# Differential attention: the heads' split on GpSimd, the second projection spread over two more softmax steps, finished heads turned first, turns two units apart

## The chip, the cores and the metric

The kernel runs on one core of a Trainium2 chip. The core has five engines with queues of their own: TensorE (PE; its weight loads are shown apart as PEld), VectorE (DVE), ScalarE (ACT), GpSimd (POOL) and SyncE (SP), and 16 DMA engines. The metric is the time of one execution on the device in microseconds; the time of a kernel is the median of its runs, and beside it one execution is profiled.

## The reference

A trunk of four layers over 512 tokens of width 1024 in fp32. The mixers are S5, gated linear attention, differential attention and S5 again; behind each stands a SwiGLU feed-forward network, and each block begins with an RMS norm. Only the third mixer, differential attention, is touched here:

```python
def diff_attn_mixer(h, positions, w_qkv, lam_q1, lam_k1, lam_q2, lam_k2, subln_g, w_o, lambda_init):
    q, k, v = jnp.split(h @ w_qkv, 3, axis=-1)
    q = partial_rope(q.reshape(bsz, seq, 2 * DIFF_HEADS, DIFF_HD), positions) * DIFF_HD ** -0.5
    k = partial_rope(k.reshape(bsz, seq, 2 * DIFF_HEADS, DIFF_HD), positions)
    v = v.astype(f32).reshape(bsz, seq, DIFF_HEADS, 2 * DIFF_HD)
    ...
        s = jnp.einsum('bqhd,bkhd->bhqk', qb, k)
        mask = chunk_id[:, None, None, :] <= qcid[:, None, :, None]
        p = jax.nn.softmax(jnp.where(mask, s, NEG_INF), axis=-1)
        p = p.reshape(bsz, DIFF_HEADS, 2, Q_BLOCK, seq)
        a = p[:, :, 0] - lam * p[:, :, 1]
        return jnp.einsum('bhqk,bkhd->bqhd', a, v)
    ...
    o = o * lax.rsqrt(jnp.mean(o * o, axis=-1, keepdims=True) + 1e-5) * subln_g.astype(f32)
    o = o * (1.0 - lambda_init)
    return o.reshape(bsz, seq, D_MODEL).astype(h.dtype) @ w_o
```

There are 8 heads, each with two softmaxes over 64-wide queries and keys and one 128-wide value; four query tiles of 128 rows each.

## The kernel before, in words

**Precision.** A large matmul runs on operands that are split into a high part in fp32r and a low part, the value less its high part: `mm3` (L394 to L396) multiplies high by high, high by low and low by high into one PSUM bank. Three such matmuls of 512 columns are a *unit* here. Weights arrive by DMA in `wst`; ACT casts the high part (L366) and DVE subtracts the low part (L374), both into a buffer `whl`. There are five `whl` buffers.

**The stage.** `diff()` first projects q, k and v of heads 0 to 3 (`project(0, z)`, z = 0, 1, 2). Then 32 softmax steps follow, i = 0 to 31; `j, t = divmod(i, 4)` are the head and its query tile. On PE, whose queue takes the work in the order of the code, one step is

- `turned(i)`: four transposes aTp of the finished softmax (L2279), which ACT copies to aT (L2281);
- `prepare(j + 1)` at t = 0, which issues nothing on PE;
- `scores(i + 2)`: four matmuls into the two banks s (L2257); DVE adds the mask and takes the minimum (L2261), ACT exponentiates (L2265), DVE divides and subtracts the two softmaxes (L2267, L2268, L2272) into pr;
- a finished head's `done`, if one is due: transposes oTp (L2312), split by ACT (L514) and DVE (L515) into oT;
- some units, then `values(i)`: op (L2289), copied by ACT into o_s (L2292) and squared into `junk` (L2294), and some units more.

The units are those of `units` at first: q, k and v of heads 4 to 7, 96 in all. A finished block of q or k is scaled by ACT into qtm (L2195) and rotated by DVE (ro, L2200 to L2206), and a *turn* is queued that is due 6 units later: four transposes qTp (L2211) and ACT's copy into qk (L2212). When `units` are used up, `last` follows: columns 0 to 511 of the output projection, 32 units. Columns 512 on of the first two token tiles run behind step 31, with four weight blocks `w1` that are loaded and split in steps 26 and 29. In step i, n holds how many units run ahead of `values` and behind it.

**prepare(j + 1)** splits the queries and keys of the next head: high part by ACT (L2231), low part by DVE (L2232), into `hl`, of which there is one buffer (head 1 borrows a `whl`). Eight DMAs on POOL's queue then lay the pieces out as qs (L2239) and ks (L2240). Of qs there are two buffers; a head's qs waits until scores of the head two before it are through.

**normalised(j)**, after a head's last step: DVE makes q2 (L2301, L2302), POOL raises it to the power −1/2 (rs, L485), and DVE scales the four tiles of o_s (L2305). oTp needs these.

**back(d)** is a DMA on POOL's queue that restores half of the residual x into vall (L2340).

**Order.** PE's order is that of the code. On ACT, DVE and POOL a scheduler sets the order, and each engine works its own queue in order: what waits at its head holds all behind it. PSUM has two banks for the transposes and op (tp), two for s and four for acc.

Of the kernel before, what the change touches and what calls it, by code (L numbers as in the profile page):

```python
# [11 lines left out]
F32 = mybir.dt.float32  # L12
# [4 lines left out]
ALU = mybir.AluOpType  # L17
# [269 lines left out]
class Trunk:  # L287
# [1841 lines left out]
    def diff(self, l, left):  # L2129
        nc, i = self.nc, self.i  # L2130
        v = nc.vector
        w, wo = i["diff_w_qkv"][0], i["diff_w_o"][0]
        self.hand(mybir.EngineType.PE)
        with self.tc.tile_pool(name="diff", bufs=1) as p:
# [39 lines left out]
            queue, clock = [], [0]  # L2174

            def run(units, n=None):

                while n is None or n:
                    if next(units, units) is units:
                        break  # L2180
                    clock[0] += 1
                    while queue and queue[0][0] <= clock[0]:
                        queue.pop(0)[1]()
                    n = n and n - 1

            def rest():
                while queue:
                    queue.pop(0)[1]()

            def project(hf, z):  # L2190
                qk = qks[hf]

                def evac(t, ps):
                    q = self.np_.tile([P, 512], F32, tag=("h", "hh")[t % 2], name="qtm", bufs=2)
                    nc.scalar.mul(q[:], ps[:], r[:, t : t + 1])  # L2195
                    s3 = ps[:].rearrange("p (h d) -> p h d", d=64)
                    q3 = q[:].rearrange("p (h d) -> p h d", d=64)
                    ro = p.tile([P, 2, 8, 16], F32, tag="ro", name="ro", bufs=2)
                    c2 = cos2[:, t].unsqueeze(1).broadcast_to([P, 8, 16])
                    v.tensor_tensor(ro[:, 0], s3[:, :, 0:16], c2, op=ALU.mult)  # L2200
                    for y in range(2):
                        s1 = sin2[:, t, y * 8 : y * 8 + 8].unsqueeze(1).broadcast_to([P, 8, 8])
                        v.tensor_tensor(  # L2203
                            ro[:, 1, :, y * 8 : y * 8 + 8], s3[:, :, 8 - 8 * y : 16 - 8 * y], s1, op=ALU.mult
                        )
                    v.tensor_tensor(q3[:, :, 0:16], ro[:, 0], ro[:, 1], op=ALU.add)  # L2206

                    def turn():
                        tp = self.tp("qTp")
                        for j in range(4):  # L2210
                            nc.tensor.transpose(tp[:, j], q[:, j * P : (j + 1) * P], self.ident[:])  # L2211
                        nc.scalar.copy(qk[:, z, :, t * P : (t + 1) * P], tp[:])  # L2212

                    queue.append((clock[0] + 6, turn))

                def evac_v(t, ps):
                    nc.scalar.mul(vall[0][:, t, hf * 512 : (hf + 1) * 512], ps[:], r[:, t : t + 1])

                if z == 2 and not vall:
                    vall.append(self.xp.tile([P, NT, D], F32, tag="x", name="vall"))  # L2220
                yield from self.gemm_units(stat, w, KT, z * D + hf * 512, evac_v if z == 2 else evac)

            ready, kept = {}, {}

            def prepare(j):


                room, bufs, tag = (self.wp, 5, "whl") if j == 1 else (p, 1, "hl")
                hl = room.tile([P, 2, 2, SEQ], F32R, tag=tag, name="hl", bufs=bufs)
                src = qks[j // 4][:, :, j % 4]  # L2230
                nc.scalar.copy(hl[:, 0], src)  # L2231
                v.tensor_tensor(hl[:, 1], src, hl[:, 0].bitcast(F32), op=ALU.subtract)  # L2232
                qs = p.tile([P, 2, SEQ], F32R, tag="qs", name="qs", bufs=2)
                ks = self.wp.tile([P, 2, 2, SEQ], F32R, tag="whl", name="ks", bufs=5)
                for m in range(2):
                    rows = slice(m * 64, (m + 1) * 64)
                    for z in range(2):
                        to = slice(z * 64, (z + 1) * 64)
                        self.nc.gpsimd.dma_start(qs[to, m], hl[rows, z, 0])  # L2239
                        self.nc.gpsimd.dma_start(ks[to, m], hl[rows, :, 1])  # L2240
                ready[j] = qs, ks
                st = self.sp.tile([P, 2, NT], F32, tag="st", name="st")
                o_s = p.tile([P, NT, P], F32, tag="o_s", name="o_s", bufs=2)
                kept[j] = st, o_s
# [30 lines left out]
            def turned(i):  # L2275
                a = soft.pop(i)
                tp = self.tp("aTp")
                for kt in range(4):
                    nc.tensor.transpose(tp[:, kt], a[:, kt * P : (kt + 1) * P], self.ident[:])  # L2279
                aT = p.tile([P, 4, P], F32, tag="aT", name="aT", bufs=2)  # L2280
                nc.scalar.copy(aT[:], tp[:])  # L2281
                return aT
# [37 lines left out]
            units = project(0, 0)  # L2320
            run(units)
            tables()
            units = project(0, 1)
            run(units)
            units = project(0, 2)
            run(units, 8)
            rest()
            prepare(0)
            run(units)

            def projections():
                for z in range(3):
                    yield from project(1, z)
# [4 lines left out]
            def back(d):  # L2338

                nc.gpsimd.dma_start(vall[0][:, :, d * 512 : (d + 1) * 512], xdv[:, :, d * 512 : (d + 1) * 512])  # L2340
# [6 lines left out]
            units, last = projections(), self.gemm_units(so, wo, KT, 0, evac0)  # L2347
            done, w1 = {}, []
# [4 lines left out]
            run(units, 2)  # L2353
            for i in range(32):
                j, t = divmod(i, NT)
                if i == 15:
                    run(units)
                    rest()
                src, n = (units, (3, 3)) if i < 15 else (last, (1, 1))
                if i in (15, 28, 31):  # L2360
                    n = (0, 0)
                elif i == 29:
                    n = (0, 2)
                aT = turned(i)
                if t == 0 and j < 7:
                    prepare(j + 1)
                if i < 30:
                    scores(i + 2)
                if i in done:
                    done.pop(i)()  # L2370
                run(src, n[0])
                values(i, aT)
                run(src, n[1])
                if i in (16, 31):
                    back(i // 31)
                if i in (26, 29):
                    w1 += [self.wb(wo, kb, 512) for kb in ((0, 2) if i == 26 else (4, 6))]
                if t == 3:
                    done[i + (2 if j in (6, 7) else 3)] = normalised(j)
            self.x = vall[0]  # L2380
# [95 lines left out]
```

## Time and profile before

| | |
|---|---|
| median of 3 runs | 2307.91 us (2306.17 to 2310.44) |
| the profiled execution | 2306.32 us |
| its span in the profile | 2304.6 us |
| the 32 softmax steps | from 1248.95 us on; step 31 begins at 1417.97 us |
| granted clock in the stage | 1.00 |

Times within the profile count from the start of the span, in us. A row of the timeline gives start, duration, engine, line, operation and tiles; brackets at its end give how long the engine stood idle before it and what ended that. The beginnings of the aTp rows mark the steps; a step is as long as PE needs for its matmuls and for what it has to wait for.

### The profile page before, as it was taken

How to read it: one execution, taken by the hardware profiler on the slowest of the kernel's cores; microseconds unless marked ns; L12 is line 12 of the kernel's file. 1: busy time of each engine (PE TensorE's matmuls, PEld its weight loads, DVE VectorE, ACT ScalarE, POOL GpSimd, SP SyncE). 2: the span in 40 equal slices, each digit the busy share in tenths (PEclk: the TensorE clock that was granted, in tenths of full speed). 3: DMA queues.
4: the chain of work that ended last, by engine and by line, in shares of the span. 5: the costliest groups of instructions: out<-in, count | busy, mean ns of one | idle time of the engine just before them, and what ended most of it. 6: DMA issues, size and time to landing. Idle time of an engine off the chain costs nothing. (4 is left out here: it accounts for less than half of the span.)

```text
span 2304.6 us, 37230 instructions
## 1 busy us (share of the span) xinstructions
PE 2218.9 (96%) x14847; PEld 1967.2 (85%) x14847; DVE 1569.8 (68%) x2430; ACT 1120.4 (49%) x1865; POOL 280.3 (12%) x386
## 2 busy tenths in 40 slices
PE   5889999999999999999999999999999899999997
PEld 3778979898877799998987787999999788989996
DVE  7873887776624469777745675876766964967674
ACT  5634645454452456555535675744534224635342
POOL 1000140512000010101002131111000100101000
PEclk8999999999999999999999999999999899999999
DMA  4246666664422457766337365886641546767521
GB/s 86 40 111 187 142 179 167 173 170 110 120 74 73 130 140 191 188 160 174 92 115 154 89 147 148 212 224 144 167 100 46 144 143 162 178 170 171 155 78 64
DMA packets 295319, 317.83 MB, mean 138 GB/s; under 512 B 72205, under 2 KB 235337, under 8 KB 294890
## 3 DMA queue, kind: packets, MB, share of 16 engines
q1 hardware_dynamic: 232906, 234.23, 34.1%
q0 software_dynamic: 62240, 81.22, 19.1%
q8 instruction: 117, 1.92, 0.4%
q14 instruction: 56, 0.46, 0.1%
HBM read 283.54 MB, written 16.65 MB: 130 GB/s over the span
## 5 line engine op out<-in xcount | busy, mean ns | idle before, releaser
L374 DVE TENSOR_TENSOR whl<-wst,whl 128x1024 fp32r<-128x1024 f32 x272 | 331.4, 1222 | 255.7 <-ACT whl L366 254.7
L366 ACT CAST whl<-wst 128x1024 fp32r<-128x1024 f32 x272 | 284.0, 1050 | 316.4 <-PE acc L396 227.8
L561 PE MATMUL a<-side,whl 128*128 128x256 f32 x3168 | 382.9, 277 | 4.0 <-DVE whl L374 3.0
L561 PEld LDWEIGHTS a<-side,whl 128*128 128x128 f32 x3168 | 370.3, 188 | 6.3 <-DVE whl L374 4.1
L394 PE MATMUL acc<-whl,act 128*128 128x512 f32 x704 | 278.3, 396 | 1.4 <-DVE x L544 1.4
L396 PE MATMUL acc<-whl,act 128*128 128x512 f32 x704 | 274.7, 390 | 0.0
L395 PE MATMUL acc<-whl,act 128*128 128x512 f32 x704 | 274.6, 390 | 0.0
L561 PE MATMUL c<-side,whl 128*128 128x256 f32 x2112 | 254.0, 277 | 1.2 <-DVE whl L374 1.2
L561 PEld LDWEIGHTS c<-side,whl 128*128 128x128 f32 x2112 | 246.6, 188 | 1.8 <-DVE whl L374 1.8
L374 DVE TENSOR_TENSOR whl<-slot,whl 128x1024 fp32r<-128x1024 f32 x107 | 130.5, 1222 | 70.1 <-ACT whl L366 70.1
L394 PEld LDWEIGHTS acc<-whl,act 128*128 128x128 f32 x704 | 132.1, 188 | 31.7 <-issue 2.7
L396 PEld LDWEIGHTS acc<-whl,act 128*128 128x128 f32 x704 | 132.1, 188 | 28.1
L395 PEld LDWEIGHTS acc<-whl,act 128*128 128x128 f32 x704 | 132.2, 188 | 25.6
L366 ACT CAST whl<-slot 128x1024 fp32r<-128x1024 f32 x107 | 112.2, 1053 | 85.1 <-PE acc L396 35.2
L394 PE MATMUL acc<-whl,hT 128*128 128x512 f32 x352 | 143.0, 406 | 2.5 <-DVE ro L2203 1.5
L395 PE MATMUL acc<-whl,hT 128*128 128x512 f32 x352 | 138.0, 392 | 0.9 <-DVE whl L374 0.9
L396 PE MATMUL acc<-whl,hT 128*128 128x512 f32 x352 | 138.0, 392 | 0.0
L561 PE MATMUL a<-sides,whl 128*128 128x256 f32 x1056 | 134.4, 283 | 0.0
L561 PE MATMUL d<-sides,whl 128*128 128x256 f32 x1056 | 132.8, 282 | 1.0 <-ACT whl L366 1.0
L561 PEld LDWEIGHTS a<-sides,whl 128*128 128x128 f32 x1056 | 129.7, 191 | 1.1
L561 PEld LDWEIGHTS d<-sides,whl 128*128 128x128 f32 x1056 | 128.7, 191 | 1.2 <-ACT whl L366 1.2
L700 ACT CAST act<-r 128x512 fp32r<-128x512 f32 (+1 forms) x110 | 66.3, 645 | 114.1 <-DVE r L679 107.6
(452 smaller groups left out, 3892.3 us busy)
## 6 DMA issues: line engine op xcount, KB each, us to landing
wst<-in_ffn_w_gate_up_dram SPq DMA_DIRECT2D x88, 512.0 KB, 4.6
wst<-in_ffn_w_down_dram SPq DMA_DIRECT2D x88, 512.0 KB, 4.4
slot<-in_ffn_w_gate_up_dram SPq DMA_DIRECT2D x71, 512.0 KB, 5.5
wst<-in_ffn_w_gate_up_dram POOLq DMA_DIRECT2D x44, 512.0 KB, 6.3
halves<-in_ffn_w_gate_up_dram SPq DMA_DIRECT2D x43, 512.0 KB, 5.1
wst<-in_s_w_glu_dram SPq DMA_DIRECT2D x32, 512.0 KB, 4.6
wst<-in_gla_w_in_dram SPq DMA_DIRECT2D x24, 512.0 KB, 3.7
wst<-in_diff_w_qkv_dram SPq DMA_DIRECT2D x24, 512.0 KB, 3.9
```

Source lines behind the costliest of these rows:

```text
L366: self.last["high"] = self.nc.scalar.copy(hl[:, 0], w[:])
L374: self.last["low"] = self.nc.vector.tensor_tensor(hl[:, 1], w[:], hl[:, 0].bitcast(F32), op=ALU.subtract)
L394: mm(out, lh, rh, start=first, stop=False)
L395: mm(out, lh, rl, start=False, stop=False)
L396: self.last["mm"] = mm(out, ll, rh, start=False, stop=last)
L561: mm(o, hl[:, x, k, c], side[:, y, k], start=first and not (j or k or n), stop=k == 3 and n == 2, skip_group_check=True,)
L700: self.last["act high"] = nc.scalar.copy(dst[:, 0, j], src[:, j])
```

## The change

It has six parts, all in `diff()`:

1. In `prepare` the high and the low part of a head's queries and keys are made by GpSimd (a cast and a subtraction of 128x1024 each) and no longer by ACT and DVE.
2. The low parts of the four weight blocks `w1` are made by GpSimd (L2387 of the changed kernel), no longer by DVE; their high parts stay with ACT.
3. The units of the second projection reach to step 15 where they ended in step 14: six a step through step 8, then five (steps 9 to 11), four (12 to 14), and five in step 15.
4. In step 3, four of the six units run ahead of `scores(5)`, the other two behind `values(3)`.
5. A finished head's `done` runs ahead of `turned(i)`, no longer behind `scores`.
6. The turns of heads 4 to 7 are due 6 + t units later, where t is the token tile, and no longer all 6 later: they lie two units apart.

```diff
-                    queue.append((clock[0] + 6, turn))
+                    queue.append((clock[0] + 6 + hf * t, turn))
...
-                nc.scalar.copy(hl[:, 0], src)
-                v.tensor_tensor(hl[:, 1], src, hl[:, 0].bitcast(F32), op=ALU.subtract)
+                nc.gpsimd.tensor_copy(hl[:, 0], src)
+                nc.gpsimd.tensor_tensor(hl[:, 1], src, hl[:, 0].bitcast(F32), op=ALU.subtract)
...
-                if i == 15:
+                if i == 16:
                     run(units)
                     rest()
-                src, n = (units, (3, 3)) if i < 15 else (last, (1, 1))
-                if i in (15, 28, 31):
+                src, n = (units, (3, 3)) if i < 16 else (last, (1, 1))
+                if i in (28, 31):
                     n = (0, 0)
                 elif i == 29:
                     n = (0, 2)
+                elif 9 <= i < 12:
+                    n = (3, 2)
+                elif 12 <= i < 15:
+                    n = (2, 2)
+                if i in done:
+                    done.pop(i)()
                 aT = turned(i)
                 if t == 0 and j < 7:
                     prepare(j + 1)
+                if i == 3:
+                    run(src, 4)
+                    n = (0, 2)
                 if i < 30:
                     scores(i + 2)
-                if i in done:
-                    done.pop(i)()
                 run(src, n[0])
                 values(i, aT)
                 run(src, n[1])
                 if i in (16, 31):
                     back(i // 31)
                 if i in (26, 29):
-                    w1 += [self.wb(wo, kb, 512) for kb in ((0, 2) if i == 26 else (4, 6))]
+                    for kb in (0, 2) if i == 26 else (4, 6):
+                        w = self.staged(self.wb_src(wo, kb, 512), 2, 512)
+                        w1.append(self.high(w, 2, 512))
+                        nc.gpsimd.tensor_tensor(w1[-1][:, 1], w[:], w1[-1][:, 0].bitcast(F32), op=ALU.subtract)
```

How the change moves instructions is seen in three places. The first is POOL's queue around steps 16 to 24, before. Here rs_12716 and rs_12913 are the powers of heads 3 and 4, hl_12926 and hl_13119 the splits of heads 6 and 7; vall is back(0).

```order
L2340 DMA vall_11409<-xkeep_11055 128x4x512
L485 TENSOR_TENSOR rs_12716<-q2_12713,mhalf_83 128x4
L2240 DMA ks_12930<-hl_12926 64x2x512 x2
L2239 DMA qs_12929<-hl_12926 64x512 x3
L2240 DMA ks_12930<-hl_12926 64x2x512
L2239 DMA qs_12929<-hl_12926 64x512
L2240 DMA ks_12930<-hl_12926 64x2x512
L485 TENSOR_TENSOR rs_12913<-q2_12910,mhalf_83 128x4
L2240 DMA ks_13123<-hl_13119 64x2x512
```

The same place in the changed kernel:

```order
L2231 CAST hl_12926<-qk_11050 128x1024
L2340 DMA vall_11409<-xkeep_11055 128x4x512
L485 TENSOR_TENSOR rs_12716<-q2_12713,mhalf_83 128x4
L2232 TENSOR_TENSOR hl_12926<-qk_11050,hl_12926 128x1024
L2240 DMA ks_12930<-hl_12926 64x2x512 x2
L2239 DMA qs_12929<-hl_12926 64x512 x3
L2240 DMA ks_12930<-hl_12926 64x2x512
L2239 DMA qs_12929<-hl_12926 64x512
L2240 DMA ks_12930<-hl_12926 64x2x512
L2231 CAST hl_13119<-qk_11050 128x1024
L2232 TENSOR_TENSOR hl_13119<-qk_11050,hl_13119 128x1024
L485 TENSOR_TENSOR rs_12913<-q2_12910,mhalf_83 128x4
```

The power of head 4, rs_12913, stood directly behind the DMAs of head 6; it now stands behind the split of head 7 as well, whose cast needs the one buffer hl, and so the end of head 6's transfers. On DVE nothing moves around what uses rs_12913: the softmax of step 21 ends with L2272, then come the four L2305, then the L2261 of step 22, in both kernels.

The second is ACT's queue in step 3, before: junk of step 2, then the cast for head 2, aT of step 3 and the evacuations of the projection.

```order
L2294 ACTIVATE junk_11820,st_11480<-op_11814 128x128
L2231 CAST hl_12209<-qk_11049 128x1024
L2281 COPY aT_11836<-aTp_11831 128x512
L2265 ACTIVATE pr_11845,st_11673<-pr_11845,nm_11846 128x512
L2265 ACTIVATE pr_11849,sums_11838<-pr_11849,nm_11850 128x512
L2195 ACTIVATE qtm_11859<-acc_11573,rcol_10777 128x512
```

And in the changed kernel:

```order
L2294 ACTIVATE junk_11820,st_11480<-op_11814 128x128
L2281 COPY aT_11836<-aTp_11831 128x512
L2195 ACTIVATE qtm_11841<-acc_11573,rcol_10777 128x512
L2195 ACTIVATE qtm_11851<-acc_11574,rcol_10777 128x512
L2195 ACTIVATE qtm_11861<-acc_11575,rcol_10777 128x512
L2195 ACTIVATE qtm_11871<-acc_11576,rcol_10777 128x512
```

The cast of hl is gone from ACT, and the evacuations come ahead of the exponentials of `scores(5)`.

The third is PE's queue at step 29, before, from its aTp to the first unit on the oT of head 6:

```order
L2279 MATMUL aTp<-ident,pr 128x128 x4
L2257 MATMUL s<-ks,qs 128x512 x4
L2312 MATMUL oTp<-ident,o_s 128x128 x4
L2289 MATMUL op<-vall,aT 128x128 x4
L394 MATMUL acc_13454<-whl,oT_13047 128x512
```

And in the changed kernel:

```order
L2312 MATMUL oTp<-ident,o_s 128x128 x4
L2279 MATMUL aTp<-ident,pr 128x128 x4
L2257 MATMUL s<-ks,qs 128x512 x4
L2289 MATMUL op<-vall,aT 128x128 x4
L394 MATMUL acc_13454<-whl,oT_13022 128x512
```

The head's transposes oTp moved from behind the scores to the step's front.

## The prediction

> **What bounds the kernel now.** I read the page first: its span, and the busy time of each engine.
>
> ```profile
> span 2304.6 us, 37230 instructions
> PE 2218.9 (96%) x14847; PEld 1967.2 (85%) x14847; DVE 1569.8 (68%) x2430; ACT 1120.4 (49%) x1865; POOL 280.3 (12%) x386
> ```
>
> TensorE is busy for 96% of 2304.6 us, and the change takes no matmul away. It touches only the 32 softmax steps of the attention layer, so I asked for the busy time by stretch: steps 0 to 15, 16 to 22 and 23 to 30. The columns are the length, then busy time (count) of PE, PEld, DVE, ACT and POOL, then the granted clock, DMA share and GB/s.
>
> ```profile
> core 0: us, PE busy (x) PEld busy (x) DVE busy (x) ACT busy (x) POOL busy (x), PEclk, DMA share, GB/s
> 1248.95:1354.70 105.75, 101.34 (x559) 85.23 (x558) 66.03 (x181) 67.07 (x163) 22.15 (x35) 1.00 0.53 115
> 1354.70:1382.93 28.23, 27.02 (x165) 22.65 (x163) 25.54 (x70) 23.15 (x67) 12.24 (x19) 1.00 0.74 161
> 1382.93:1417.97 35.04, 30.37 (x175) 23.89 (x175) 25.27 (x69) 23.21 (x66) 2.82 (x2) 1.00 0.35 97
> ```
>
> The lengths less PE's busy time are 4.41, 1.21 and 4.67 us: about 10.3 us in which PE stands still, 0.45% of the run, at a granted clock of 1.00. In the middle stretch DVE is busy for 25.54 of 28.23 us, so what holds DVE there soon holds PE.
>
> Next I read PE's timeline. Every step begins with the four transposes aTp, so their starts T(i) cut the stage into steps. The columns are start, duration, engine, line, output and inputs; in brackets the idle time before and what ended it.
>
> ```profile
> 1261.69 0.60 PE L2279 MATMUL aTp<-ident,pr 128*128 128x128 f32 x4
> 1268.08 0.60 PE L2279 MATMUL aTp<-ident,pr 128*128 128x128 f32 x4
> 1272.14 1.16 PE L2289 MATMUL op<-vall,aT 128*128 128x128 f32 x8 [0.50 <-ACT aT L2281]
> 1275.47 0.48 PE L394 MATMUL acc<-whl,hT 128*128 128x512 f32 x1 [1.48 <-DVE ro L2203]
> 1277.38 0.60 PE L2279 MATMUL aTp<-ident,pr 128*128 128x128 f32 x4
> 1283.48 1.16 PE L2289 MATMUL op<-vall,aT 128*128 128x128 f32 x8 [1.17 <-ACT qk L2212]
> 1346.62 0.60 PE L2279 MATMUL aTp<-ident,pr 128*128 128x128 f32 x4
> 1351.93 0.66 PE L2279 MATMUL aTp<-ident,pr 128*128 128x128 f32 x4 [1.07 <-DVE oT L515]
> 1354.70 0.60 PE L2279 MATMUL aTp<-ident,pr 128*128 128x128 f32 x4
> 1358.34 0.60 PE L2279 MATMUL aTp<-ident,pr 128*128 128x128 f32 x4
> 1361.98 0.60 PE L2279 MATMUL aTp<-ident,pr 128*128 128x128 f32 x4
> 1382.93 0.65 PE L2279 MATMUL aTp<-ident,pr 128*128 128x128 f32 x4 [0.23 <-ACT junk L2294]
> 1397.28 0.50 PE L394 MATMUL acc<-whl,oT 128*128 128x512 f32 x1 [0.68 <-ACT oT L514]
> 1398.56 0.50 PE L396 MATMUL acc<-whl,oT 128*128 128x512 f32 x1 [0.55 <-DVE oT L515]
> 1406.89 0.60 PE L2279 MATMUL aTp<-ident,pr 128*128 128x128 f32 x4
> 1413.18 0.50 PE L394 MATMUL acc<-whl,oT 128*128 128x512 f32 x1 [1.67 <-ACT oT L514]
> 1414.94 0.60 PE L2279 MATMUL aTp<-ident,pr 128*128 128x128 f32 x4
> ```
>
> A step with six units takes 6.39 us (1261.69 to 1268.08, i=2), one with two 3.64 (1358.34 to 1361.98, i=17): 0.69 a unit, 2.27 without. A qTp or oTp adds about 0.35, by estimate from its four transposes. Against that, step 3 (1268.08 to 1277.38, one turn) is 9.30 − 6.74 = 2.6 too long, step 14 (1346.62 to 1351.93, two units, one oTp) 1.3, step 15 (no unit) 0.5, and step 29 (1406.89 to 1414.94) 8.05 − 3.99 = 4.1. Step 4 waits 1.17 for qk copies, step 26 0.68 + 0.55 for an oT.
>
> **The split on GpSimd: what it frees.** The casts of the split, on ACT, before:
>
> ```profile
> 1270.56 1.05 ACT L2231 CAST hl<-qk 128x1024 fp32r<-128x1024 f32 x1 [3.81 <-DMA ks<-hl]
> 1320.79 1.05 ACT L2231 CAST hl<-qk 128x1024 fp32r<-128x1024 f32 x1
> 1334.85 1.06 ACT L2231 CAST hl<-qk 128x1024 fp32r<-128x1024 f32 x1 [2.29 <-DMA ks<-hl]
> 1370.91 1.05 ACT L2231 CAST hl<-qk 128x1024 fp32r<-128x1024 f32 x1 [1.01 <-DMA ks<-hl]
> ```
>
> There is one hl buffer, so a head's cast waits until the transfers of the head before have landed, and ACT waits with it. At 1270.56 that was 3.81 us: aT, the evacuations qtm and DVE's ro queue behind it, and this is PE's 0.50 + 1.48 in step 3. On POOL the wait holds none of them. With the four units ahead of scores(5), I take 2.3 off step 3 (bounds 0 and 2.6) and 1.2 off step 4, where the cast and the copies share ACT.
>
> **Units and turns.** Five units now stand in step 15, fewer in steps 9 to 14; units only move. Step 15 then covers the 1.07 wait and the 0.5, and step 14 its 1.3: I take 1.6. So T(16) would come 2.3 + 1.2 + 1.6 = 5.1 us before 1354.70, at 1349.6.
>
> **The split on GpSimd: what it costs.** The rows nearest to the new work are these. The first three are groups (busy us, mean ns); the others are single instructions of POOL and DVE.
>
> ```profile
> L2232 DVE TENSOR_TENSOR hl<-qk,hl 128x1024 fp32r<-128x1024 f32 x7 | 8.5, 1222 | 3.1 <-ACT hl L2231 3.1
> L1882 POOL MEMSET wa<- 128x512 f32 x1 | 0.5, 527 | 0.0
> L1028 POOL TENSOR_SCALAR nident<-ident 128x128 fp32r<-128x128 f32 x1 | 0.5, 544 | 0.0
> 1277.30 1.22 DVE L374 TENSOR_TENSOR whl<-wst,whl 128x1024 fp32r<-128x1024 f32 x1
> 1277.54 2.07 POOL L485 TENSOR_TENSOR rs<-q,mhalf 128x4 f32<-128x4 f32 x1 [15.92 <-DVE q L2302]
> 1305.16 1.03 POOL L485 TENSOR_TENSOR rs<-q,mhalf 128x4 f32<-128x4 f32 x1 [12.01 <-DVE q L2302]
> 1322.13 1.10 POOL L2239 DMA_DIRECT2D qs<-hl  x2 [15.94 <-ACT hl L2231]
> 1355.79 0.80 POOL L2340 DMA_DIRECT2D vall<-xkeep  x1 [10.84 <-PE s L2257]
> 1357.92 1.22 POOL L2240 DMA_DIRECT2D ks<-hl  x2
> 1370.25 1.43 POOL L485 TENSOR_TENSOR rs<-q,mhalf 128x4 f32<-128x4 f32 x1 [6.82 <-DVE q L2302]
> 1371.71 1.14 DVE L2305 SCALAR_TENSOR_TENSOR o_s<-o_s,rs,sg 128x128 f32<-128x128 f32 x4 [0.93 <-POOL rs L485]
> 1372.77 0.69 DVE L2261 CUSTOM_DVE_ANT_0 pr<-s,mask 128x512 f32<-128x512 f32 x1
> 1376.11 0.75 DVE L2272 SCALAR_TENSOR_TENSOR pr<-pr,sums 128x512 f32<-128x512 f32 x1
> ```
>
> POOL shows no cast and no subtraction of 128x1024. From below both are bounded by the engines that do them now, 1.05 (the ACT rows above) and 1.22; from above by the fp32r operation of POOL, 0.544 for 128 columns, times eight: 4.35 each. MEMSET passes 512 columns in 0.527, so 1024 in 1.05. The operand shape is nearest to that row: I take 1.2 for the cast (one stream in), and 2.4 for the subtraction, which reads two (2 × 1.05, and 0.3 for waits at the ports); 3.6 a head. [...]
>
> Now POOL's chain through the second half. A head's eight transfers need 12.7 us from the first issue to the last landing (1322.13 to the cast released at 1334.85; the later pair 1357.92 and 1370.91 gives 13.0). The chain starts with the last qk turn. Before, it stood at the end of step 9, and the cast followed its copy at 1320.79. In the change it comes after the first three units of step 10: that step starts some 4.5 us sooner (2.3 + 1.2, and one unit and one turn fewer in step 9), and aTp, scores(12), three units, the turn and its copy take as long by estimate, so that the copy ends at about the same 1320.8. Then: split of head 4 to 1324.4; landed 1337.1; split of head 5 to 1340.7; landed 1353.4; cast of head 6, back(0) 0.80, rs of head 3 1.03 and the subtraction, 5.4 in all, to 1358.8; landed 1371.5; split of head 7 to 1375.1. Only then comes rs of head 4, since POOL's order puts it behind that split: to 1376.2. DVE's four L2305 wait for it: to 1377.3, where they ended at 1372.85 before. On DVE the softmax of step 22 (L2261) is queued behind them; from its start to the finished pr it took 4.1 us (1372.77 to 1376.86), with a split of 1.22 between that is gone; I take 4.0. So T(22) is 1381.3, and T(23), a step of 3.64 + 0.35 on, 1385.3 against 1382.93: **+2.4**. What step 3, step 4, the spread units and steps 20 to 22 win lies ahead of this wait and is swallowed by it: the chain starts at a time they don't move. scores(16), in step 14, needs head 4 by about 1339.3 and has it at 1337.1.
>
> **Behind the wait.** w1's four subtractions (L2387) leave DVE for a POOL that is idle then (2.82 of 35.04 us busy). In step 26 the finished head is turned first, so its oT is ready sooner: −1.2, the two waits. In step 29 the same, and the two L374 ahead of L515 are gone: of 4.1 us I take 1.6 (bounds 0 and 3.5), since aTp now needs a bank that ACT's junk frees. Sum: +2.4 − 1.2 − 1.6 = −0.4, so 2305.9 on the profiled execution's 2306.32. The median is 1.6 higher than that execution: 2307.5, say **2307**.
>
> **Rivals.** (a) *POOL is quick.* If cast and subtraction cost 2.3 together, the lower bound, the four heads bring the chain forward by 4 × 1.3 = 5.2; if its landings are some 1.3 shorter, 4 more. The whole chain slack gone, all gains count: 5.1 in steps 3 to 15, 1.2 in steps 16 to 22 (all that PE stands still there, 28.23 − 27.02), 2.8 behind: −9.1, 2299. With the price alone, 2302. For it: DVE itself does the subtraction in 1.22. Against it: 0.544 for 128 columns on POOL.
>
> (b) *POOL and DVE hold each other.* The trace shows it: the rs of 1277.54 took 2.07, not 1.03, as if its own 1.03 began when the L374 of 1277.30 ended, at 1278.52; the rs of 1370.25 took 1.43. Eight long POOL operations in the second half, beside a DVE that is busy for 25.54 of 28.23 us, would each lose 0.4 to 1.0: 3 to 8 us on the same chain, and DVE's own operations (pr in L2272) stand up to 2.4 behind a subtraction. At 5.1 a head in place of 3.6 the chain is 6 us longer: 2313. It is slower than before from about 4.85 a head on. [...] Against it: the rs of 1305.16 ran its 1.03 unhindered, so POOL and DVE don't always meet.
>
> (c) *The change does less than it says.* If the new order wins nothing in steps 26 and 29 (a bank of PSUM takes the place of oT), 2.8 is missing: 2310. It stays within the same bound as the forecast, and I count it there.
>
> **How the numbers follow.** A difference of 0.2%, 4.6 us, is about what a measurement of this kernel can tell from no change. Forecast with (c), 2303.3 to 2312.5: 0.42. Rival (a), 2299 to 2303: 0.34, since the price of POOL is the widest unknown and leans on no row of the same shape. Rival (b), 2312.5 and up: 0.24. The likeliest case's own range is 2303 to 2312; the range that holds the time 8 times in 10 takes in most of (a) and (b): 2297 to 2315.
>
> **What would show it.** Right: T(4) − T(3) near 7, T(16) near 1350, then PE waiting in steps 20 to 22 for s or pr, with DVE's L2305 waiting some 5 us for rs, and POOL's row for rs directly behind a subtraction of hl. Wrong: POOL's two operations under 2.6 or over 4.9 together, or a step 22 that starts before 1375; also a wait of scores(16) for transfers in step 14, or one for the finished head that moves rather than ends in step 29.

## The result and the profile after

The changed kernel takes 2330.56 us (median of 6 runs, 2323.15 to 2334.76) against 2308.26 us before: a ratio of 1.0093, 95% interval 1.0078 to 1.0107. It is 22 us slower, outside the forecast range. Its profiled execution took 2330.14 us. The page of the changed kernel, span and busy time:

```profile
span 2328.4 us, 37204 instructions
PE 2227.8 (96%) x14847; PEld 1973.9 (85%) x14847; DVE 1575.1 (68%) x2418; ACT 1113.9 (48%) x1857; POOL 319.2 (14%) x406
```

PE has the same 14847 matmuls. The same three stretches as in the prediction, steps 0 to 15, 16 to 22 and 23 to 30, of the changed kernel:

```profile
core 0: us, PE busy (x) PEld busy (x) DVE busy (x) ACT busy (x) POOL busy (x), PEclk, DMA share, GB/s
1249.94:1365.38 115.44, 103.92 (x560) 87.24 (x558) 68.35 (x181) 64.17 (x162) 37.30 (x50) 0.96 0.58 114
1365.38:1402.67 37.29, 30.05 (x164) 24.93 (x163) 25.57 (x58) 20.18 (x56) 21.46 (x24) 0.86 0.74 158
1402.67:1443.81 41.14, 32.84 (x175) 26.05 (x174) 29.43 (x71) 25.13 (x73) 10.02 (x5) 0.92 0.21 62
```

They are 9.7, 9.1 and 6.1 us longer than before, 24.9 in all: the stage accounts for the whole loss (the spans differ by 23.8). POOL is busy for 21.46 of 37.29 us in the middle where it was busy for 12.24 of 28.23, and the granted clock, 1.00 before, fell to 0.86. By the starts of aTp, the steps that moved are (us):

| step | before | after | difference |
|---|---|---|---|
| 0 | 6.39 | 19.40 | +13.0 |
| 3 | 9.30 | 6.79 | −2.5 |
| 4 | 9.18 | 9.31 | +0.1 |
| 5 to 15 | 68.14 | 67.18 | −1.0 |
| 17 | 3.64 | 11.26 | +7.6 |
| 18 | 4.10 | 5.95 | +1.9 |
| 19 to 24 | 24.20 | 25.26 | +1.1 |
| 25 | 4.35 | 8.12 | +3.8 |
| 26, 27 | 9.49 | 7.34 | −2.2 |
| 28 | 2.77 | 7.77 | +5.0 |
| 29 | 8.05 | 6.06 | −2.0 |

PE's timeline of the changed kernel shows what it waited for in the steps that grew:

```profile
1263.82 2.08 PE L2289 MATMUL op<-vall,aT 128*128 128x128 f32 x8 [10.28 <-ACT aT L2281]
...
1374.72 1.17 PE L2312 MATMUL oTp<-ident,o_s 128*128 128x128 f32 x4 [1.89 <-DVE o_s L2305]
1380.29 1.11 PE L2279 MATMUL aTp<-ident,pr 128*128 128x128 f32 x4 [4.41 <-ACT junk L2294]
...
1414.07 1.34 PE L2257 MATMUL s<-ks,qs 128*128 128x512 f32 x4 [1.97 <-DVE nm L2261]
...
1431.56 1.02 PE L2312 MATMUL oTp<-ident,o_s 128*128 128x128 f32 x4 [1.66 <-DVE o_s L2305]
1434.73 1.12 PE L2279 MATMUL aTp<-ident,pr 128*128 128x128 f32 x4 [2.14 <-ACT junk L2294]
```

**Step 0.** PE waits 10.28 us for aT, so ACT was late. ACT's row, and POOL's queue ahead of it:

```profile
1262.23 1.04 ACT L366 CAST whl<-wst 128x1024 fp32r<-128x1024 f32 x1 [11.66 <-DMA ks<-hl]
```

```profile
1243.20 1.04 POOL L2231 CAST hl<-qk 128x1024 fp32r<-128x1024 f32 x1 [12.13 <-DMA ks<-hl]
1244.33 2.39 POOL L2232 TENSOR_TENSOR hl<-qk,hl 128x1024 fp32r<-128x1024 f32 x1
1246.66 1.50 POOL L2231 CAST hl<-qk 128x1024 fp32r<-128x1024 f32 x1
1248.24 2.40 POOL L2232 TENSOR_TENSOR hl<-qk,hl 128x1024 fp32r<-128x1024 f32 x1
1250.60 2.13 POOL L2239 DMA_DIRECT2D qs<-hl  x4
```

ACT wants to cast a weight block into a `whl` buffer, and that buffer is the one that head 1 borrowed for its split: it is free only when head 1's eight transfers have landed. In POOL's queue the split of head 2 stands ahead of that of head 1. The cast of head 2 needs the one buffer hl, so it waits for head 0's transfers (12.13 us), and head 1's split and transfers stand behind it. Head 1's transfers begin at 1250.60. The order is not new: before, ACT made the two casts in one go, the first behind the same landing.

```profile
1237.49 2.00 ACT L2231 CAST hl<-qk 128x1024 fp32r<-128x1024 f32 x2 [2.16 <-DMA ks<-hl]
```

Head 1's transfers began 2.3 us behind that, at 1239.78. In the changed kernel head 0 lands 5.7 us later (1243.20), and POOL works 7.4 us on the two splits behind the landing, so head 1's transfers begin 10.8 us later in all.

**Steps 17 and 18.** POOL's and DVE's rows there:

```profile
1369.13 1.04 POOL L2231 CAST hl<-qk 128x1024 fp32r<-128x1024 f32 x1 [5.56 <-DMA ks<-hl]
...
1371.04 1.05 POOL L485 TENSOR_TENSOR rs<-q,mhalf 128x4 f32<-128x4 f32 x1
1372.07 2.34 POOL L2232 TENSOR_TENSOR hl<-qk,hl 128x1024 fp32r<-128x1024 f32 x1
```

```profile
1372.12 3.24 DVE L2305 SCALAR_TENSOR_TENSOR o_s<-o_s,rs,sg 128x128 f32<-128x128 f32 x4 [4.33 <-POOL rs L485]
...
1391.87 1.14 DVE L2305 SCALAR_TENSOR_TENSOR o_s<-o_s,rs,sg 128x128 f32<-128x128 f32 x4 [0.93 <-POOL rs L485]
...
1410.15 3.25 DVE L2305 SCALAR_TENSOR_TENSOR o_s<-o_s,rs,sg 128x128 f32<-128x128 f32 x4 [0.94 <-POOL rs L485]
...
1428.99 3.21 DVE L2305 SCALAR_TENSOR_TENSOR o_s<-o_s,rs,sg 128x128 f32<-128x128 f32 x4 [0.90 <-POOL rs L485]
```

The power of head 3 stands behind the cast of head 6, which waited 5.56 us for a landing; DVE waits 4.33 us for the power. Then its four L2305 take 3.24 us in place of 1.14: POOL has begun the subtraction of head 6 0.05 us before. The difference, 2.1, is nearly all of that subtraction. Behind L2305 stand the softmaxes: ACT's exponential waits 7.73 us for nm, and junk, which frees the bank for aTp, is queued behind it.

```profile
1378.30 0.72 ACT L2265 ACTIVATE pr<-pr,nm 128x512 f32<-128x512 f32 x1 [7.73 <-DVE nm L2261]
```

In steps 25 and 28 L2305 takes 3.2 again, each time right behind a power that a subtraction of w1 follows:

```profile
1408.62 1.50 POOL L485 TENSOR_TENSOR rs<-q,mhalf 128x4 f32<-128x4 f32 x1 [8.23 <-DVE q L2302]
1410.10 2.36 POOL L2387 TENSOR_TENSOR whl<-wst,whl 128x1024 fp32r<-128x1024 f32 x1
```

The L2305 at 1391.87, with no subtraction behind its power, takes 1.14. Of the 3.8 and 5.0 us that steps 25 and 28 lose, 1.4 and 3.0 belong to the new order (e2_order below).

### The profile page after: what moved, and what is told of

It is laid out like the page before. It is cut to its first block, busy times and chain, and to the rows that moved or that the text cites. A ratio compares the mean times of both kernels' runs of the same rounds, so it can differ in the third digit from the quotient of the medians.

```text
span 2328.4 us, 37204 instructions
## 1 busy us (share of the span) xinstructions
PE 2227.8 (96%) x14847; PEld 1973.9 (85%) x14847; DVE 1575.1 (68%) x2418; ACT 1113.9 (48%) x1857; POOL 319.2 (14%) x406
## 4 chain that ended last, share of the span: by engine, by line
PE 80%; DVE 8%; issue 4%; DMA 3%; ACT 3%; POOL 1%; SPq 1%; ACTq 0%; DVEq 0%; POOLq 0%
PE a L561 18%; PE acc L394 13%; PE acc L396 13%; PE acc L395 12%; PE c L561 9%; PE d L561 5%; PE y L1470 2%; DVE whl L374 2%; DMA ks<-hl 2%; PE V L1434 1%; PE tp L123 1%; PE op L2289 1%; ACT whl L366 1%; PE s L2257 1%; PE y L1468 1%
## 5 line engine op out<-in xcount | busy, mean ns | idle before, releaser
L374 DVE TENSOR_TENSOR whl<-wst,whl 128x1024 fp32r<-128x1024 f32 x268 | 329.3, 1233 | 268.4 <-ACT whl L366 267.5
L374 DVE TENSOR_TENSOR whl<-slot,whl 128x1024 fp32r<-128x1024 f32 x107 | 130.4, 1222 | 70.2 <-ACT whl L366 70.2
```

Source lines behind the costliest of these rows:

```text
L374: self.last["low"] = self.nc.vector.tensor_tensor(hl[:, 1], w[:], hl[:, 0].bitcast(F32), op=ALU.subtract)
```

## The experiments

Step 0 began between 1247.8 and 1258.0 us in the profiled executions, so the table goes by stretches: from the start of step 0 to that of step 16 (105.75 us before) and on to that of step 31 (63.27 before). The stretches are those of the profiled execution, which can lie some us from the median of its run (e3_split: 2322.9 against 2329.5). Ratios are against runs of the kernel before on the same chip; medians of different runs come from different chips. A row's line numbers are those of its own kernel, a few lines off from run to run.

| run | median, us | ratio (95%) | steps 0 to 15 | steps 16 to 30 |
|---|---|---|---|---|
| the change | 2330.6 | 1.0093 (1.0078 to 1.0107) | +9.7 | +15.2 |
| e1_heads012 | 2321.7 | 1.0066 (1.0047 to 1.0086) | −4.6 | +16.0 |
| e2_order | 2305.4 | 0.9995 (0.9982 to 1.0009) | −2.7 | −0.4 |
| e3_split | 2329.5 | 1.0094 (1.0071 to 1.0118) | +11.9 | +6.7 |
| e4_w1 | 2312.4 | 1.0019 (1.0006 to 1.0031) | −1.1 | +5.4 |
| e5_not_head2 | 2325.4 | 1.0067 (1.0051 to 1.0084) | −4.0 | +16.7 |
| e6_no_power | 2326.1 | 1.0066 (1.0049 to 1.0083) | +8.3 | +12.1 |
| e7_one_input | 2329.5 | 1.0088 (1.0070 to 1.0106) | +9.1 | +15.1 |
| b1_heads34 | 2308.4 | 0.9996 (0.9986 to 1.0006) | +1.9 | −0.7 |
| c4_w1_back | 2311.5 | 1.0017 (1.0007 to 1.0028) | −4.1 | +8.9 |
| c1_cast_only | 2303.2 | 0.9980 (0.9968 to 0.9992) | −5.1 | +1.3 |
| c3_heads345 | 2309.2 | 1.0002 (0.9991 to 1.0013) | −4.6 | +5.5 |
| b5_head3 | 2304.5 | 0.9983 (0.9973 to 0.9993) | −2.9 | −2.2 |
| f1_cast_mid | 2305.2 | 0.9974 (0.9963 to 0.9985) | −4.7 | +0.9 |
| f2_no_power | 2305.3 | 0.9982 (0.9969 to 0.9995) | −5.1 | −0.2 |
| f3_cast_all | 2306.8 | 0.9984 (0.9975 to 0.9993) | −3.7 | +0.3 |

### Which part loses

Heads 0 to 2 off GpSimd:

```diff
-                nc.gpsimd.tensor_copy(hl[:, 0], src)
-                nc.gpsimd.tensor_tensor(hl[:, 1], src, hl[:, 0].bitcast(F32), op=ALU.subtract)
+                if j > 2:
+                    nc.gpsimd.tensor_copy(hl[:, 0], src)
+                    nc.gpsimd.tensor_tensor(hl[:, 1], src, hl[:, 0].bitcast(F32), op=ALU.subtract)
+                else:
+                    nc.scalar.copy(hl[:, 0], src)
+                    v.tensor_tensor(hl[:, 1], src, hl[:, 0].bitcast(F32), op=ALU.subtract)
```

> The changed kernel with the splits of heads 0, 1 and 2 back on ACT and DVE; heads 3 to 7 and w1 stay on GpSimd. Theory P (POOL's queue and port): the 10.3 us wait in step 0 comes from POOL's order, in which the cast of head 2 waits for the landing of head 0 and holds the split and the transfers of head 1, whose buffer ACT's next weight cast needs. Then step 0 is about 6.4 us again and the run some 13 us shorter than the changed kernel: 2315 to 2319. Rival: the stall is one of the weight transfers or of the turns, and stays: 2328 to 2332.

Step 0 is 6.35 us, the stall is gone, and the stage is 13.5 us shorter than that of the change. The time came out 2.7 us above P's range, far from the rival's. The second half is as long as in the changed kernel.

The order alone (both pairs of GpSimd lines back on ACT and DVE):

> The changed kernel with all splits and w1's low parts back on ACT and DVE: only the spread units, the four units ahead of scores(5), the earlier done and the turns two apart are left. Theory P: all losses come from GpSimd; without them the new order wins something of the waits in steps 3, 14, 15, 26 and 29: 2299 to 2304. Rival R (the order loses): the transposes of a finished head now stand ahead of aTp, so that a late o_s or a bank held by junk stops PE in steps 18, 26 and 29; then 2309 to 2318.

2305.4, between the two ranges and not to be told from the kernel before; the stage is 3.1 us shorter. R falls: oTp ahead of aTp does cost 1.3, 1.4 and 3.0 us in steps 17, 25 and 28, but steps 26 and 29 give more than that back (−2.2 and −4.3; step 18 gives 0.4). P was right that the losses come from GpSimd; it expected somewhat more from the order.

The splits alone, in the order of before:

> The kernel before with nothing changed but the splits of all heads on GpSimd; w1 stays on DVE, the order is that of before. Theory P: the 13 us of step 0 come back in full, and DVE's L2305 of head 3 or 4 waits for its power behind a split, some 3 to 8 us more: 2322 to 2330. Rival R: step 0 alone, 2319 to 2322, and L2305 takes 1.14 for four.

As P said, 2329.5. Step 0 takes 18.81 us, and later aTp waits 1.80 and 3.32 us for pr: the losses of GpSimd don't need the new order. The second of these waits, in step 21, is the one that the prediction had named: the power of head 4 stands on POOL behind the split of head 7 and three of its DMAs, and DVE waits for it.

```profile
1390.51 1.14 DVE L2305 SCALAR_TENSOR_TENSOR o_s<-o_s,rs,sg 128x128 f32<-128x128 f32 x4 [4.28 <-POOL rs L485]
```

No L2305 of heads 0 to 6 meets a subtraction in this run: each four take 1.14. Step 3 is only 0.2 us shorter than before, where the order alone won 1.5 and both together 2.5.

w1 alone, in the order of before:

> The kernel before with nothing changed but w1's four low parts on GpSimd. Theory P: the subtraction that follows a head's power on POOL takes the port just as DVE's L2305 begins: the four L2305 of heads 5 and 6 take 3.3 us in place of 1.14, and the run is 2 to 7 us longer: 2310 to 2315. Rival: DVE is freed of four L374 of 1.22 and nothing is held: 2304 to 2308, with L2305 at 1.14.

2312.4, as P said. The kernel with w1 alone on GpSimd, DVE's rows and POOL's:

```profile
1392.12 3.25 DVE L2305 SCALAR_TENSOR_TENSOR o_s<-o_s,rs,sg 128x128 f32<-128x128 f32 x4 [0.93 <-POOL rs L485]
```

```profile
1392.08 2.36 POOL L2380 TENSOR_TENSOR whl<-wst,whl 128x1024 fp32r<-128x1024 f32 x1
```

The subtraction begins 0.04 us ahead of L2305, and L2305 waits it out. For the next head it is the same (3.22 us, the subtraction 0.06 ahead). Four subtractions of 1.22 taken off DVE cost 5.4 us in this stretch.

### Step 0: the order on POOL or the length

Only head 2's split taken off GpSimd (`if j != 2:` in the diff above):

> The changed kernel with only the split of head 2 back on ACT and DVE. Theory P1: in the changed kernel POOL's queue has the cast of head 2 ahead of the split of head 1, and it waits there for the landing of head 0. With head 2 gone from POOL, head 1's split runs as soon as head 0's transfers are issued, its transfers follow, and the 10.3 us wait of step 0 vanishes as it did with three heads back: T(1) - T(0) near 6.4, the stage about 13 us shorter, 2315 to 2322. Rival P2: POOL is simply slow for three splits early on (each 3.5 us where ACT and DVE take 2.3); then about 4 of the 13 us are won, and step 0 still waits 5 us or more: 2325 to 2329.

Step 0 is 6.38 us: with head 2 gone from POOL's queue there is no stall, as P1 said. But the time, 2325.4, lies above its range and in that of P2, whose condition, a wait of 5 us or more left in step 0, isn't met. The cast of head 2 waits 7.5 us for head 0's landing on ACT now, and holds what is queued there. PE's row ahead of step 0, outside the stretches of the table (before, the same wait was 0.43):

```profile
1247.64 0.50 PE L394 MATMUL acc<-whl,hT 128*128 128x512 f32 x1 [3.70 <-ACT vall L2217]
```

Casts of all heads on GpSimd, all subtractions on DVE, w1 as before:

```diff
-                nc.gpsimd.tensor_tensor(hl[:, 1], src, hl[:, 0].bitcast(F32), op=ALU.subtract)
+                v.tensor_tensor(hl[:, 1], src, hl[:, 0].bitcast(F32), op=ALU.subtract)
```

> The changed kernel with GpSimd making the casts of all heads, 0 to 2 too, and all subtractions and w1 on ACT and DVE. POOL's order still has the cast of head 2, waiting for the landing of head 0, ahead of head 1's. If the order is the cause: head 0's landing comes some 2 us later than in the kernel before, where the same wait took ACT's cast to 1237.5, so step 0 loses little or nothing, 0 to 4 us, against 13, since the two subtractions of 2.4 and the 3.3 of head 0 are gone from the chain. If it's the order alone and not the length: a wait of 5 us or more stays in step 0. Time 2303 to 2307 in the first case, 2309 to 2314 in the second.

POOL's order is that of the change, head 2's cast ahead of head 1's. Step 0 is 7.22 us, 0.8 over before where it was 13 over, and the time, 2306.8, is that of the first case. So it takes both: the order, which the kernel before has too, puts head 0's landing ahead of head 1's transfers, and the subtractions on POOL (3.27 for head 0, 2.39 and 2.40 for the next two) make that chain long enough to reach ACT.

### The second half: the wait for the power and the held DVE

The power left out:

```diff
-                rs = self.rsqrt(q2[:], NT, 0.0)
+                rs = q2
```

> The changed kernel without the power of each head (rs on POOL): DVE's L2305 scales by q2 itself, so this part of the computation is left out, and DVE waits for nothing on POOL. Step 0 stays as it is (10.3). Theory P3, that both the wait for rs and the port cost time: the 4.3 us wait of L2305 for rs in step 17 is gone, and with it the chance that L2305 and a POOL subtraction start together; steps 17 to 19, 25 and 28 win 10 to 12 us together: 2317 to 2322. Rival (the wait for rs is harmless, PE stops for banks and the new order): 2327 to 2331.

2326.1 lies between the two ranges. Only 3 us came back from step 16 on, and P3 had said 10 to 12. Step 17 is 7.62 us long in place of 11.26, so the wait for the power is worth 3.6 there. But other operations of DVE now meet the subtraction. In this run:

```profile
1370.96 3.88 DVE L374 TENSOR_TENSOR whl<-wst,whl 128x1024 fp32r<-128x1024 f32 x1
```

```profile
1371.36 2.39 POOL L2232 TENSOR_TENSOR hl<-qk,hl 128x1024 fp32r<-128x1024 f32 x1
```

An L374 that takes 1.22 alone took 3.88: it ended 1.1 behind the subtraction, though by its row it had begun 0.4 ahead of it, while POOL issued back(0). Three of the L2305 still took 3.2 (heads 4 to 6).

One operand fewer in L2305:

```diff
-                    v.scalar_tensor_tensor(
-                        o_s[:, t], o_s[:, t], rs[:, t : t + 1], sg[:], op0=ALU.mult, op1=ALU.mult
-                    )
+                    v.tensor_scalar(o_s[:, t], o_s[:, t], rs[:, t : t + 1], None, op0=ALU.mult)
```

> The changed kernel with sg left out of L2305: o_s times rs alone, one operand from SBUF and a scalar, where there were two operands (the gain is left out of the computation). Theory P4, that a POOL subtraction holds a DVE operation with two SBUF operands: the four L2305 that took 3.24 where a subtraction began just ahead of them take 1.1 or less, the wait for rs in step 17 stays (4.3), and steps 17, 25 and 28 win 2 us each: 2322 to 2327. Rival: one operand is held just as long, about 3.2, and the time stays: 2328 to 2332.

```profile
1370.80 2.98 DVE L2305 TENSOR_SCALAR o_s<-o_s,rs 128x128 f32<-128x128 f32 x4 [4.33 <-POOL rs L485]
...
1390.54 0.88 DVE L2305 TENSOR_SCALAR o_s<-o_s,rs 128x128 f32<-128x128 f32 x4 [0.93 <-POOL rs L485]
```

P4 falls: with one 128x128 operand from SBUF, and the scalar rs, it is held just as long (2.98 against 0.88 unhindered), and the time stays. Two full operands are not needed for DVE to be held.

The next three go step by step from e1 to the order alone. First w1 back on DVE:

> The changed kernel with the splits of heads 0 to 2 and w1's low parts back on ACT and DVE; cast and subtraction of heads 3 to 7 stay on GpSimd. From step 16 to step 31 the run with w1 still on GpSimd was 16.0 us longer than the kernel before. Theory (the port is held for every POOL subtraction, and each collision costs about its 2.4 us): w1's share there, some 5 to 7 us, is gone, and what is left lies in steps 17 to 22: the stretch is 9 to 11 us longer than before, the run 2313 to 2318. Rival: the losses of steps 25 and 28 belong to the new place of the finished head and stay: 2318 to 2323.

From step 16 on +8.9 in place of +16.0: w1's share is 7.1 us. The rival falls: steps 25 and 28 are 1.3 and 3.0 us over before, as with the order alone, and were 3.9 and 5.1 over. The time, 2311.5, is below the expected range. Then the subtractions of heads 3 to 7 back on DVE, the casts left on GpSimd:

> As the run with heads 3 to 7 on GpSimd and w1 on DVE, but GpSimd makes only the casts of these heads; their subtractions are back on DVE. POOL's order is the same, with the power of head 3 still behind the cast of head 6, which waits for a landing. Theory P5 (the held port is half of what is left): no L2305 and no L374 takes over 1.3 for want of the port beyond a cast's 1.0; the wait for the power in step 17 stays, 3 to 4 us; the stretch from step 16 to 31 is 3 to 5 us longer than before, the run 2306 to 2311. Rival (the wait for the power is all of it): the stretch is 8 us or more longer, 2312 to 2317.

+1.3 in place of +8.9, and 2303.2 us, under P5's range: faster than both kernels. With the casts alone, DVE's operations are as long as before the change (L2309 is L2305 of the changed kernel, L2233 the subtraction):

```profile
L2309 DVE SCALAR_TENSOR_TENSOR o_s<-o_s,rs,sg 128x128 f32<-128x128 f32 x32 | 9.3, 347 | 6.8 <-POOL rs L485 6.8
L2233 DVE TENSOR_TENSOR hl<-qk,hl 128x1024 fp32r<-128x1024 f32 x5 | 6.1, 1225 | 9.1 <-POOL hl L2232 9.1
L2232 POOL CAST hl<-qk 128x1024 fp32r<-128x1024 f32 x5 | 5.2, 1038 | 47.0 <-DMA ks<-hl 28.4 <-ACT qk L2212 18.6
```

The wait of 3 to 4 us for the power that P5 expected to stay was gone as well: POOL's chain is shorter by its subtractions, and the cast of head 6 no longer comes late enough to hold the power of head 3. DVE waits 9.1 us for these five casts in all, since the next operation in its queue is the subtraction that needs the cast; through the cast of 1369.01 (1.04) it stands idle, from 1368.82 to 1370.09.

The power left out where only the splits of heads 3 to 7 are on GpSimd (the diff of the power above, on top of c4):

> The changed kernel with heads 0 to 2 and w1 back on ACT and DVE, and without the power of each head (L2305 scales by q2: this part of the computation is left out). With the power the stretch from step 16 to 31 was 8.9 us longer than before. If the wait for the power is the main part, 5 us or more go: 2304 to 2307. If the held port is: 1 to 3 us go, and an L374 or L2272 takes over 2 us in place of the L2305 that took 3.24: 2308 to 2311.

−0.2 in place of +8.9: nine us came back, so here the wait for the power was the main part, although an L374 was held (3.59 us). Without the power L2305 also starts earlier, and no longer right beside the subtraction that held it; what that alone is worth this run doesn't show. Step 17 alone, in us, by what is on GpSimd:

| run | step 17 |
|---|---|
| w1 back, splits of heads 3 to 7 on GpSimd | 11.35 |
| the same without the power | 7.33 |
| the casts alone on GpSimd | 6.10 |
| the new order alone | 4.97 |
| the kernel before | 3.64 |

Read as steps from one row to the next, the wait for the power is about 4.0 us of it, the subtraction beside DVE 1.2, the casts 1.1, the new place of the finished head 1.3. Over the whole second half the parts don't add up (the power gave 3 us with w1 on GpSimd and 9 without), and what decides there which operation meets a subtraction is left open.

### Versions that keep what won

Heads 3 and 4 on GpSimd, a finished head turned first from step 26 on only:

> A combination: of the change the spread units, the four units ahead of scores(5) and the turns two apart; the splits of heads 3 and 4 alone on GpSimd, those of all others and w1's low parts on ACT and DVE; a finished head turned first from step 26 on only. By the step lengths so far: -2.5 in step 3, -0.6 in step 4, -2 in steps 9 to 15, -2 in steps 26 to 30, together some 6 us under the kernel before: 2300 to 2304. Rival: what is won in the first half is lost again behind step 16, as in the run with the order alone: 2305 to 2309.

2308.4, in the rival's range, but not by its mechanism: nothing is lost behind step 16 (−0.7). Step 14 took 11.09 us in place of 5.31. Heads 3, 4 and 5 on GpSimd:

> The changed kernel with GpSimd splitting heads 3, 4 and 5 alone; all other splits and w1 on ACT and DVE. The power of head 3 then stands behind no waiting cast. Theory: the stall of step 17 (7.6 us) is gone from POOL; but ACT's cast of head 6 now waits for head 5's landing in its place, which comes some 4 us later than before, and aT queues behind it: 2 to 4 us in steps 14 to 17; 2305 to 2310. Rival: ACT has room there and the gain of the first half (4.6 us) stays: 2302 to 2305.

The theory holds, with 6.5 us in step 16 where it had 2 to 4. In the first run ACT's casts wait 7.4 us for landings, six casts together, in the second 8.0, four together. By the theory the largest of these waits is that of the first head that is back there, for the landing of one that GpSimd split late, and aT or junk stands behind it. PE's rows, of the run with heads 3 and 4 and of that with 3 to 5:

```profile
1349.65 0.66 PE L2316 MATMUL oTp<-ident,o_s 128*128 128x128 f32 x4 [3.29 <-ACT junk L2298]
```

```profile
1361.79 2.08 PE L2293 MATMUL op<-vall,aT 128*128 128x128 f32 x8 [4.74 <-ACT aT L2285]
```

Head 3 alone on GpSimd:

> A combination: of the change the spread units, the four units ahead of scores(5) and the turns two apart; only head 3 split on GpSimd, all else on ACT and DVE; a finished head turned first except in steps 16 to 25. By the step lengths so far: the order alone won 3.1 us in the stage, head 3 on GpSimd adds 0.7 to 1, and the heads of steps 18 and 22 turned behind the scores as before add 1.5: some 5 us under the kernel before, 2302 to 2305. Rival: a wait moves, as in the combination with heads 3 and 4, and nothing is left of it: 2306 to 2310.

2304.5, a ratio of 0.9983: five us off the stage, as expected. Casts alone with the older place of the finished head in steps 16 to 25:

> The run with GpSimd making only the casts of heads 3 to 7, and a finished head turned behind the scores as before in steps 16 to 25 (heads 3 and 4), ahead of aTp elsewhere. If the earlier place still costs something there (steps 17 and 21 were 2.5 and 2.0 us longer than before, steps 18, 20 and 22 shorter, 1.8 in sum): 2300 to 2303. If the sum of 1.8 us comes from elsewhere: 2303 to 2306, as the run without this.

The stage is 3.85 us shorter than before, as with the casts alone (3.85), so this place costs nothing that can be told: the 0.4 us that steps 16 to 30 win are no more than what steps 0 to 15, whose code is the same in both runs, lose. Both versions beat the kernel before by 0.2% to 0.3%.

## Why the prediction was wrong

**The wait that POOL was to take.** "On POOL the wait holds none of them" was the step that cost most, 13.0 of 24.9 us. I followed the splits from step 3 on and put nothing down for heads 0 to 2. There the wait for a landing holds head 1's transfers, as it did before, and they hold a weight buffer that ACT needs. With the longer splits on POOL the transfers began 10.8 us later, and the wait came back to ACT through the shared buffer (11.66 us). The runs show that it takes the subtractions on POOL and this order together.

**The chain.** The prices were right: 1.04 to 1.1 for the cast (1.2 taken), 2.38 for the subtraction (2.4 taken), 1.95 times DVE's 1.22. The 0.3 for waits at the ports within that 2.4 was an estimate that no run shows by itself; where DVE's L2272 ran beside the cast at 1246.66, POOL's row was 1.50 long, 0.46 more than the 1.04. The transfers took 10 to 17 us from the first issue to the last landing (1359.13 to the cast released at 1369.13, 1226.49 to that at 1243.20; 12.7 taken). That a power would come late behind a split and hold DVE's softmax was right in kind, but I named head 4's, and in the changed kernel it was head 3's (4.33 us); head 4's was late in the order of before (4.28). Head 3's stands in the prediction's own sum: landed 1353.4, then 1.2, 0.80 and 1.03, so it ends at 1356.4, 6.8 us behind its T(16) of 1349.6. In the changed kernel L2305 began 6.7 behind T(16), before 3.3 behind it. So the time was right, and the wait that follows from it was put at nothing: L2305 comes forward with T(16), and the power could not. The cast that holds it is only the first half of a split, and a wait for a landing stands ahead of it.

**The port.** The time lies where rival (b) put it, 2312.5 and up, but only in part for its reason: the stall of step 0 and the wait for the power come from POOL's queue. Rival (b) let POOL lose 0.4 to 1.0 an operation; that was seen (3.27 in place of 2.39 on head 0's subtraction), but beside it DVE was held for nearly the whole subtraction, 2.1 us on four L2305, three times. Its sentence on the L2272 behind a subtraction ("up to 2.4") had the right size and was not taken into the sum. No run shows what all these holds cost together. The rows show which operations were held: L2305 with two full operands and with one (3.24 and 2.98 us for 1.14 and 0.88), L374 (3.88 for 1.22) and L2272 (1.43 for 0.75, below); L2261, with an operand in PSUM (below), was not (0.69). What the two engines share, the "port" of the prediction and the expectations, no run shows, nor which operand decides. One kind of row stands apart: the L374 of 3.88 us began 0.4 ahead of the subtraction, while POOL issued a DMA, and was held all the same.

**w1.** "For a POOL that is idle then" counted POOL's time and not its place in the queue: two of the four subtractions follow a power directly, and the first operation that the power releases is the one they hold. Expected: a part of a gain of 1.6; measured: a loss of 7.1 (5.4 in the order of before).

**What was right.** Step 3 won 2.5 (2.3 forecast). Step 4 won 0.6 with heads 0 to 2 off GpSimd (1.2 forecast), nothing in the change itself. The spread units and the turns: steps 5 to 15 won 1.5 in that same run (1.6 forecast). Steps 25 to 30 won 2.1 in the run with the order alone (2.8 forecast, by the same two places). So T(16) does come 4.6 us sooner without the stall (5.1 forecast). That all of this would be swallowed was right as well, and it was swallowed by more than a wait of 2.4. One word ahead of the prediction has to be put right: the cast in ACT's queue at step 3 (hl_12209) is that of head 3, not head 2.

## What to carry to other kernels

Work that is moved to an idle engine has to be followed in that engine's queue from its first instruction to its last: what now stands behind a wait there, which transfers among it, and which buffers those free. Compare the new time of a signal with when its consumer wants it in the changed kernel, not in the old one. Of the split here, the cast with its one input was the part to move to GpSimd (1.04 against 1.05 on ACT; 2303.2 us with the casts alone) and the subtraction with its two the part to leave on VectorE (2.38 against 1.22; 2311.5 us with both moved), above all not right behind a signal that VectorE waits for (3.24 for 1.14). The shorter one can hold VectorE too: in the changed kernel an addition that began 0.1 us behind a cast (POOL, 1285.62, 1.04 us) took 1.08 us in place of 0.28.

```profile
1285.73 1.08 DVE L2206 TENSOR_TENSOR qtm<-ro 128x128 f32<-128x128 f32 x1
```

## What the hardware showed that I had not expected

A DVE operation can be held to the end of a GpSimd subtraction of 128x1024 that it meets, and this was seen for SCALAR_TENSOR_TENSOR, TENSOR_TENSOR and TENSOR_SCALAR on SBUF (3.24, 3.88 and 2.98 us for 1.14, 1.22 and 0.88). It doesn't hold for all. Within the subtraction of 1244.33 (shown above) a TENSOR_SCALAR on one column ran its usual 0.27, and the L2272 behind it was held, 1.43 for 0.75:

```profile
1245.53 0.27 DVE L2268 TENSOR_SCALAR sums<-st,sums,neglam 128x1 f32<-128x1 f32 x1
1245.84 1.43 DVE L2272 SCALAR_TENSOR_TENSOR pr<-pr,sums 128x512 f32<-128x512 f32 x1
```

And an L2261, which reads s from PSUM and the mask from SBUF, ran at its usual 0.69 within a subtraction:

```profile
1387.79 2.38 POOL L2232 TENSOR_TENSOR hl<-qk,hl 128x1024 fp32r<-128x1024 f32 x1
```

```profile
1387.95 0.69 DVE L2261 CUSTOM_DVE_ANT_0 pr<-s,mask 128x512 f32<-128x512 f32 x1
```

And the stall of step 0 cost more than its length: TensorE's granted clock fell. The changed kernel's stretches around the stall of step 0 (same columns as above):

```profile
1253.00:1263.80 10.80, 0.53 (x3) 0.11 (x1) 1.48 (x4) 1.57 (x3) 2.10 (x4) 0.77 0.98 174
1263.80:1266.00 2.20, 2.18 (x9) 2.19 (x10) 1.45 (x4) 1.45 (x5) 0.00 (x0) 0.50 0.20 30
1266.00:1269.00 3.00, 3.00 (x8) 2.32 (x8) 0.47 (x1) 0.47 (x3) 0.00 (x0) 0.50 0.41 153
1269.30:1275.00 5.70, 5.70 (x32) 4.90 (x31) 3.58 (x9) 3.59 (x9) 3.84 (x8) 1.00 0.50 88
```

For some 5 us behind 10.3 us without work the clock is 0.50, and a matmul of 512 columns takes 0.63 in place of 0.39. From op to the next aTp step 0 takes 5.52 us in place of 2.95, which is most of the 2.7 by which it grew beyond the wait itself. The same view gives 0.50 for 1374.92 to 1385.15 (steps 17 and 18) and 1432.94 to 1439.77 (steps 28 and 29) too, so part of what these steps lost is the clock; how much no run separates. In the stall of step 0 the same view shows 1.00 up to 1258, some 4.5 us behind PE's last matmul, and 0.50 from 1259 on; from 1269.3 on it is 1.00 again, 5.5 us behind the op of 1263.82. Which wait of PE is long enough to lower the clock no run shows.
